# The last group of a split-fp32 down-projection: 28 additions moved from VectorE to transfers that add in SBUF

## The chip, the cores and the metric

The kernel runs on one core of one Trainium2 chip. A core has TensorE (matmuls, with a weight load per matmul), VectorE (elementwise work), ScalarE (activations, here mostly copies with a scale), GpSimd, SyncE (which here only issues transfers) and 16 DMA engines shared by all queues. The metric is the device time of one execution in microseconds.

## The reference, cut to what matters

One layer of a hybrid streaming encoder is computed for 512 prompt frames and 64 sample frames: a mixer, an output projection with a gated residual, and a gated feed-forward network (FFN) with its own gated residual, then a final norm. The change lies in the last three lines:

```python
x = x + g1 * mix                       # D_MODEL = 2048
h = rmsnorm(x, norm2[l]) * (1 + sc2) + sh2
f, s_f = conv_ffn(h, ffn_s[l], w_up[l], ffn_conv_w[l], ffn_conv_b[l], w_down[l])
x = x + g2 * f                         # f = act @ w_down, w_down (5632, 2048)
...
y = rmsnorm(x, final_norm)
```

`g2` is one gain per model column and per stream (prompt or sample). Everything is fp32.

## The kernel before, in words

Activations lie transposed: model columns on the 128 partitions, frames along the free dimension. A tile of 128 columns is kept as two halves `h`, each of 288 frames: 256 of the prompt and 32 of the sample (`HP` = 256, `HT` = 288; `HZ` = 290 has two extra columns between them, `ZS` = 258 is where the sample begins in it). An fp32 product is made of three matmuls: each operand is split into a high part (a copy by ScalarE to a rounded type) and a low part (the difference, by VectorE), and high x high, low x high and high x low are added up in PSUM.

**The norm stage** (lines 1190 to 1208). The first residual `x` is finished tile by tile while the output projection goes on. For each of the 16 tiles `norm_tile` squares `x`, stores `x` to DRAM (`xd[m]`, L1204, because it is wanted again at the very end), scales `x` in place for the second norm (L1206, ScalarE; this must wait for the store, which reads the same tile) and has GpSimd put two columns in the gap (L1207). The up-projection begins right behind the last tile; its first product is copied out by L1385 into `p`.

**The down-projection** multiplies `act` (44 tiles of 128 rows) by `w_down` (5632 x 2048). The first two of the 44 tiles go through plain products that also set the accumulators; the next 38 are paired and go through a Strassen-like scheme with 7 products instead of 8; the last four ("plain activations") go through plain products in `final`. The 38 make 19 pairs in 5 groups (3, 4, 4, 4, 4). A group has 4 blocks `q`, each of 512 of the 2048 output columns (two tiles of row half 0, two of row half 1), and each block has 7 steps `c`. A step of a group of four is 24 matmuls.

`down_prep` makes the weight split of a step two steps ahead: L1557 (ScalarE, high) and L1558 (VectorE, low), with sums of weight tiles before it on VectorE (L1551, L1568, L1578, L1583). Weights are loaded by SyncE (L1533) into six buffers used in turn, so a load waits until the split of the tile six loads before is made. The split tiles have three buffers in turn. After a step `down_out` adds the product from PSUM to an accumulator: to `acc[row, h][q]` (quarters of 128 x 2 x 288), or to `e0[q]` for product 0 (L1621 where it comes from two single banks, L1623 otherwise).

`e0` belongs in three of the four accumulators, so in the last group it is added to (1,1), (0,1) and (1,0) of each block by VectorE (L1698), after steps 1, 2 and 3. Then `down_finish` turns an accumulator into the new `x`: its pieces of the old `x` are loaded from `xd` (four issues, L1630), it is scaled by the gain `g2` on ScalarE (four activations, L1634), and the loaded `x` is added by VectorE (L1636). The four `(row, h)` of a block are begun after steps 1 to 4 of the block and added after its steps 4 to 7. The stage buffers for the loaded `x` and for the last plain activations are four tiles of the up-projection in turn (`stage`).

The last four plain activations are loaded (L1478) after step 4 of each block of the last group and split (L1484 ScalarE, L1485 VectorE) after step 6, so in steps 6, 13, 20 and 27 of the 28.

**The final part** begins right after step 27: for each half `h` and each of 16 tiles `m`, 12 matmuls with the last plain activations (L561, L563). Weight tiles come through the same six buffers and three split buffers for `m` below 6 (L648 load, L649, L650) and into free tiles above (L1780, L1783, L1784). `final_sum` (L1737, VectorE) adds the product with the gain to `x`; after every fourth tile `final_part` transposes the result on TensorE (L1810) and makes the last norm.

The order of instructions on each engine follows the program's order, changed by a planner of the framework that picks among ready instructions by the order of the program and by its own cost estimates; a few loads have a priority written by hand. `events[n]` in `down` is a list of calls made after step `n`.

Of the kernel before, what the change touches and what calls it, by code (L numbers as in the profile page):

```python
# [8 lines left out]
F32 = mybir.dt.float32  # L9
F32R = mybir.dt.float32r  # L10
I32 = mybir.dt.int32
AF = mybir.ActivationFunctionType
ALU = mybir.AluOpType
# [3 lines left out]
P = 128  # L17
D = 2048
KD = 16
TP, TS = 512, 64  # L20

HP, HS, HT = 256, 32, 288
NFF = 44
# [4 lines left out]
HZ, ZS = 290, 258  # L28
# [73 lines left out]
class Kern:  # L102
# [1091 lines left out]
    def norm_tile(self, m, first):  # L1194

        nc = self.nc
        A, x = nc.scalar, self.x1[m]
        if first:
            A.activation(self.sq, x, AF.Square)
        else:  # L1200
            t = self.xr()[:, :2 * HZ].rearrange("p (h t) -> p h t", h=2)
            A.activation(t, x, AF.Square)
            nc.vector.tensor_tensor(self.sq, self.sq, t, op=ALU.add)
        nc.sync.dma_start(self.xd[m], x)  # L1204
        for c, q in ((slice(0, HP), 0), (slice(ZS, HZ), 1)):
            A.activation(x[:, :, c], x[:, :, c], AF.Copy, scale=self.s2[:, m, q:q + 1])  # L1206
        nc.gpsimd.tensor_copy(x[:, 0, HP:ZS], self.mod[:, 3, m])  # L1207
# [402 lines left out]
    def down_out(self, step, c):  # L1610
# [11 lines left out]
        else:  # L1622
            V.tensor_tensor(out, (x, y)[(0, 1, 2, 0, 1, 2, 1)[c]], out, op=ALU.add)  # L1623

    def down_finish(self, row, h, q):

        nc, t, xt = self.nc, self.acc[row, h][q], self.stage()
        for a in range(2):
            for c, z in ((slice(0, HP), slice(0, HP)), (slice(HP, HT), slice(ZS, HZ))):
                nc.sync.dma_start(xt[:, a, c], self.xd[8 * row + 2 * q + a][:, h, z])  # L1630
        yield
        for a in range(2):
            for n, c in enumerate((slice(0, HP), slice(HP, HT))):
                nc.scalar.activation(t[:, a, c], t[:, a, c], AF.Copy, scale=self.g2[:, 8 * row + 2 * q + a, n:n + 1])  # L1634
        yield
        nc.vector.tensor_tensor(t, t, xt, op=ALU.add)  # L1636

    def down(self):
        A = self.nc.scalar
        free = [self.combos[c, j][2] for c in range(7) for j in range(NPAIR)]  # L1640
        take = lambda n: [free.pop(0) for _ in range(n)]
        self.combos, self.a, self.n_stage = {}, {}, 0
        self.raw = self.raw_late
        firsts = take(3 * FIRST)
        loads = [self.act_load(k, firsts[k]) for k in range(FIRST)]
        self.places = firsts[FIRST:]
        acts = [self.act_split(raw) for raw in loads]
        self.places = take(7 * GROUPS[0])
        quarters = lambda places: [self.slot(p, F32, HT) for p in places]
        self.acc = {}  # L1650
        for row in range(2):
            for h in range(2):
                self.acc[row, h] = quarters(take(4))
        self.e0_places = take(4)
        self.e0 = quarters(self.e0_places)
        spare = take(2 * GROUPS[0])
        self.places += free + firsts + spare
        self.g2 = self.sp.tile([P, KD, 2], F32, tag="g2", bufs=1, name="g2")
        for half, f in ((0, 1.0), (1, -1.0)):
            A.activation(self.g2[:, 8 * half:8 * half + 8], self.mod[:, 5, 8 * half:8 * half + 8], AF.Copy, scale=f)  # L1660

        steps = [((g, q), c) for g in range(len(GROUPS)) for q in range(4) for c in range(7)]
        blocks = [b for b, c in steps if c == 0] + [None]
        prep = lambda n: self.down_prep(*steps[n], blocks[n // 7 + 1]) if n < len(steps) else None
        raws = [self.pair_load(j, spare[2 * j:]) for j in range(GROUPS[0])]
        for m0 in range(0, KD, 4):
            wh, wl = self.wtile(self.i["w_down"][0, :FIRST * P, m0 * P:(m0 + 4) * P].rearrange("(k p) n -> p k n", p=P))
            if m0 == 4:
                self.down_load(blocks[0], ("a21", "a22"))
            if m0 == 8:  # L1670
                self.down_load(blocks[0], ("a11", "a12"))
                self.down_first(blocks[0])
            for m in range(m0, m0 + 4):
                ps = self.pgt()
                c = slice((m - m0) * P, (m - m0 + 1) * P)
                for k in range(FIRST):
                    self.mm6(ps, wh[:, k, c], wl[:, k, c], acts[k], k == 0, k == FIRST - 1)
                for h in range(2):
                    A.activation(self.acc[m // 8, h][m % 8 // 2][:, m % 2], ps[:, h, :HT], AF.Copy, scale=(1.0, -1.0)[m // 8])
            j = m0 // 4  # L1680
            if j < GROUPS[0]:
                for _ in self.down_pair(j, raws[j]):
                    pass
        for n in range(2):
            prep(n)

        last, acts, pairs = len(GROUPS) - 1, [], iter(())
        puts = {2: (1,) * 7, 3: (0, 3, 4, 4, 3, 4, 3)}
        events = [[] for _ in range(len(steps) + 1)]
        for q in range(4):  # L1690
            b = 7 * (4 * last + q)
            for i, (row, h) in enumerate(((0, 0), (1, 1), (0, 1), (1, 0))):
                f = self.down_finish(row, h, q)
                for at in (1, 3, 4):
                    events[b + i + at].append(lambda f=f: next(f, None))
            for c, (row, h) in enumerate(((1, 1), (0, 1), (1, 0)), 1):
                t = self.acc[row, h][q]
                events[b + c].insert(0, lambda t=t, e=self.e0[q]: self.nc.vector.tensor_tensor(t, t, e, op=ALU.add))  # L1698
            load = []
            events[b + 4].append(lambda q=q, load=load: load.append(self.act_load(NFF - 4 + q)))  # L1700
            events[b + 6].append(lambda load=load: acts.append(self.act_split(load.pop())))
        for n, (step, c) in enumerate(steps):
            g, q = step
            prep(n + 2)
            self.down_product(step, c)
            self.down_out(step, c)
            freed = lambda c: [self.combos[c, sum(GROUPS[:g]) + i][2] for i in range(GROUPS[g])]
            if q == 3 and c > 0:
                self.places += freed(c - 1)
            if g < last:  # L1710
                if (q, c) == (1, 6):
                    pairs = self.next_pairs(range(sum(GROUPS[:g + 1]), sum(GROUPS[:g + 2])))
                    next(pairs)
                for _ in range(puts[q][c] if q in puts else 0):
                    next(pairs)
            for f in events[n]:
                f()
            if q == 3 and c == 6:
                next(pairs, None)
                self.places += freed(c)  # L1720
        for f in events[-1]:
            f()
        self.final(acts, self.places + [])
# [110 lines left out]
def layer_kernel(tc, i, o):  # L1834
    nc = tc.nc
    with ExitStack() as ctx:
        K = Kern(tc, ctx, i, o)
        pool = lambda st, name, side="left", **kw: st.enter_context(tc.tile_pool(name=name, side=side, reuse_waits="tile", **kw))
        dp = ctx.enter_context(tc.tile_pool(name="dp", bufs=1, space=DRAM))
# [7 lines left out]
        K.zero3 = K.cp.tile([P, 3], F32, name="zero3")  # L1847
        nc.vector.memset(K.zero3, 0.0)
        K.xs = [dp.tile([P, 2, HT], F32, name=f"xs{k}") for k in range(KD)]
        K.xd = [dp.tile([P, 2, HZ], F32, name=f"xd{m}") for m in range(KD)]  # L1850
        K.actd = [dp.tile([P, 2, HT], F32, name=f"actd{t}") for t in range(NFF)]
        K.hp = pool(ctx, "hp", bufs=1)
        K.wq = pool(ctx, "wq", "right", bufs=3)
        with ExitStack() as early:
# [37 lines left out]
            z = [(K.zp, f"z{n}") for n in range(N_EXTRA)]  # L1892
# [98 lines left out]
```

## Time and profile before

| | us |
|---|---|
| three runs, median (lowest to highest) | 2870.66 (2866.38 to 2871.43) |
| profiled execution, whole | 2869.18 |
| its span, first to last instruction | 2867.4 |
| down-projection, last group (28 steps) | about 2695 to 2783.5 |
| final part | about 2783.5 to the end |

An instruction row gives engine, line, operation, output <- inputs, shapes, count, then the total busy time and the mean of one in ns, then the idle time of the engine before it and what ended it. A row of a stretch gives for each engine the busy time and in brackets the number of instructions, then the clock granted to TensorE (1.00 is full), the busy share of the 16 DMA engines and the rate in GB/s. A row of a single instruction in order of time gives its start, its duration, engine and line, with the idle time before it in square brackets. A row of a wait gives who waited for whom, the total in us, how many times and the longest. Busy times of two neighbouring instructions overlap a little, so the distance between two starts is what an instruction costs its engine.

### The profile page before, as it was taken

How to read it: one execution, taken by the hardware profiler on the slowest of the kernel's cores; microseconds unless marked ns; L12 is line 12 of the kernel's file. 1: busy time of each engine (PE TensorE's matmuls, PEld its weight loads, DVE VectorE, ACT ScalarE, POOL GpSimd, SP SyncE). 2: the span in 40 equal slices, each digit the busy share in tenths (PEclk: the TensorE clock that was granted, in tenths of full speed). 3: DMA queues.
4: the chain of work that ended last, by engine and by line, in shares of the span. 5: the costliest groups of instructions: out<-in, count | busy, mean ns of one | idle time of the engine just before them, and what ended most of it. 6: DMA issues, size and time to landing. Idle time of an engine off the chain costs nothing.

```text
span 2867.4 us, 52042 instructions
## 1 busy us (share of the span) xinstructions
PE 2810.4 (98%) x20596; PEld 2708.7 (94%) x20596; DVE 2301.9 (80%) x3742; ACT 1355.0 (47%) x2379; POOL 320.6 (11%) x587
## 2 busy tenths in 40 slices
PE   7999999999999999999999999999999999999998
PEld 3599999999999999999999999999999999999997
DVE  5788878777778777468888888888887889999995
ACT  7574566544333333255444444444444464434453
POOL 0005432224310001001000000000000000000000
PEclk9999999999999999999999999999999999999999
DMA  9975555545455448433333333333333343443451
GB/s 308 306 209 148 157 149 161 158 140 152 129 166 172 146 131 251 123 119 102 102 101 102 108 106 108 102 108 108 101 101 105 105 150 114 123 127 118 126 169 67
DMA packets 522441, 399.80 MB, mean 139 GB/s; under 512 B 50793, under 2 KB 453956, under 8 KB 522196
## 3 DMA queue, kind: packets, MB, share of 16 engines
q1 hardware_dynamic: 516772, 385.79, 45.3%
q0 software_dynamic: 5424, 10.68, 1.2%
q8 instruction: 162, 2.65, 0.4%
q14 instruction: 83, 0.68, 0.1%
HBM read 356.24 MB, written 40.13 MB: 138 GB/s over the span
## 4 chain that ended last, share of the span: by engine, by line
PE 82%; DVE 9%; DMA 3%; ACT 3%; issue 2%; SPq 0%; POOL 0%; ACTq 0%; DVEq 0%
PE g L561 19%; PE g L563 10%; PE g L1373 9%; PE g L1374 8%; PE g L1375 8%; PE bank L1374 3%; PE bank L1373 3%; PE bank L1375 3%; DVE wl L1558 2%; PE g L1606 2%; PE g L1608 2%; PE g L1607 2%; DMA raw<-in_w_down_dram 1%; PE bank L162 1%; PE bank L826 1%
## 5 line engine op out<-in xcount | busy, mean ns | idle before, releaser
L1373 PE MATMUL g<-slot,wh 128*128 128x290 f32 x1760 | 534.2, 304 | 2.4 <-ACT p L1385 2.4
L1374 PE MATMUL g<-slot,wh 128*128 128x290 f32 x1760 | 526.6, 299 | 0.0
L1375 PE MATMUL g<-slot,wl 128*128 128x290 f32 x1760 | 520.9, 296 | 0.0
L561 PE MATMUL g<-hh,wh 128*128 128x288 f32 x1984 | 450.4, 307 | 2.4 <-ACT hh L1160 1.3
L561 PE MATMUL g<-hl,wh 128*128 128x288 f32 x1984 | 432.3, 298 | 0.0
L563 PE MATMUL g<-hh,wl 128*128 128x288 f32 x1984 | 432.0, 298 | 0.0
L1320 ACT ACTIVATE wh<-raw 128x1024 fp32r<-128x1024 f32 x176 | 186.8, 1061 | 393.1 <-PE g L1374 376.8
L1373 PEld LDWEIGHTS g<-slot,wh 128*128 128x128 f32 x1760 | 331.8, 189 | 16.9 <-ACT p L1385 11.3
L1375 PEld LDWEIGHTS g<-slot,wl 128*128 128x128 f32 x1760 | 337.2, 192 | 0.0
L1374 PEld LDWEIGHTS g<-slot,wh 128*128 128x128 f32 x1760 | 335.6, 191 | 0.1
L561 PEld LDWEIGHTS g<-hh,wh 128*128 128x128 f32 x1984 | 319.1, 190 | 5.6 <-ACT hh L1160 1.5
L561 PEld LDWEIGHTS g<-hl,wh 128*128 128x128 f32 x1984 | 321.3, 189 | 0.3
L563 PEld LDWEIGHTS g<-hh,wl 128*128 128x128 f32 x1984 | 319.6, 189 | 0.2 <-issue 0.2
L649 ACT ACTIVATE wh<-raw 128x1024 fp32r<-128x1024 f32 x163 | 172.6, 1059 | 309.1 <-PE g L561 272.6
L650 DVE TENSOR_TENSOR wl<-raw,wh 128x1024 fp32r<-128x1024 f32 x163 | 199.1, 1222 | 52.8 <-ACT wh L649 50.9
L820 DVE SCALAR_TENSOR_TENSOR acc<-xr,ct,acc 128x512 f32<-128x512 f32 x322 | 230.4, 751 | 1.5 <-DMA xr<-in_w_ada_dram 1.5
L1321 DVE TENSOR_TENSOR wl<-raw,wh 128x1024 fp32r<-128x1024 f32 x176 | 214.8, 1220 | 19.3 <-ACT wh L1320 19.2
L1606 PE MATMUL g<-slot,wh 128*128 128x288 f32 x760 | 224.8, 296 | 2.3 <-DVE slot L1623 1.1
L1608 PE MATMUL g<-slot,wl 128*128 128x288 f32 x760 | 224.4, 296 | 0.3 <-DVE wl L1558 0.3
L1607 PE MATMUL g<-slot,wh 128*128 128x288 f32 x760 | 224.4, 295 | 0.0
L1374 PE MATMUL bank<-slot,wh 128*128 128x290 f32 x704 | 210.3, 299 | 0.0
L1373 PE MATMUL bank<-slot,wh 128*128 128x290 f32 x704 | 209.6, 298 | 0.0
(416 smaller groups left out, 6083.0 us busy)
## 6 DMA issues: line engine op xcount, KB each, us to landing
raw<-in_w_up_dram SPq DMA_DIRECT2D x176, 512.0 KB, 4.0
raw<-in_w_in_dram SPq DMA_DIRECT2D x108, 512.0 KB, 3.9
xr<-in_w_ada_dram SPq DMA_DIRECT2D x86, 512.0 KB, 3.9
raw<-in_w_down_dram SPq DMA_DIRECT2D x76, 512.0 KB, 3.6
ax<-in_w_ada_dram SPq DMA_DIRECT2D x42, 512.0 KB, 3.7
hraw<-in_w_ada_dram SPq DMA_DIRECT2D x40, 512.0 KB, 9.5
raw<-in_w_out_dram SPq DMA_DIRECT2D x32, 512.0 KB, 4.3
raw<-in_w_ada_dram SPq DMA_DIRECT2D x24, 512.0 KB
```

The costliest lines, as they stand in the source:

```text
L561: T.matmul(ps[:, h if bank is None else bank, :n], wh, x[:, h, :n], start=f, stop=False)
L563: T.matmul(ps[:, h if bank is None else bank, :n], wl, ah[:, h, :n], start=False, stop=stop)
L650: nc.vector.tensor_tensor(lo[:, :n_], raw[:, :n_], hi[:, :n_].bitcast(F32), op=ALU.subtract)
L820: V.scalar_tensor_tensor(acc[s], w[:, k], col, acc[s], op0=ALU.mult, op1=ALU.add)
L1320: self.nc.scalar.activation(hi, src, AF.Copy)
L1321: self.nc.vector.tensor_tensor(lo, src, hi.bitcast(F32), op=ALU.subtract)
L1373: T.matmul(ps, wh[:, j], hi, start=(c < 3 and j == 0), stop=False, skip_group_check=True)
L1374: T.matmul(ps, wh[:, j], lo, start=False, stop=False, skip_group_check=True)
L1375: T.matmul(ps, wl[:, j], hi, start=False, stop=(j == NPAIR - 1), skip_group_check=True)
L1606: T.matmul(ps, wh[:, j, f], hi, start=(c < 3 and j == 0), stop=False, skip_group_check=True)
L1607: T.matmul(ps, wh[:, j, f], lo, start=False, stop=False, skip_group_check=True)
L1608: T.matmul(ps, wl[:, j, f], hi, start=False, stop=(j == n - 1), skip_group_check=True)
```

## The change

Four things change.

- `e0` and the old `x` are added to the accumulators in the last group by transfers that GpSimd issues, with addition as the operation on their target in SBUF (`down_add`). There are 12 for `e0` (after steps 0, 1 and 4 of a block: to (1,0), (0,1), (1,1)) and 16 for `x`. The additions on VectorE, the loads of `x` into stage buffers and their issues on SyncE go.
- The scaling by `g2` and the addition of `x` come after steps 3, 5, 6 and 7 of a block, for (0,0), (0,1), (1,1), (1,0); the scaling waits for the `e0` transfer, the `x` transfer for the scaling.
- The old `x` is kept in DRAM by quarters, in the layout of the accumulators, so that one transfer of 128 x 576 adds a quarter. The norm stage therefore stores each tile in four pieces (two halves, prompt and sample) instead of one.
- The last plain activations are loaded into one buffer of the up-projection (tag `g`), after steps 0, 6, 12 and 18 of the last group's 28, and split after steps 3, 9, 15 and 21.

```diff
@@ norm_tile
-        nc.sync.dma_start(self.xd[m], x)
+        for h in range(2):
+            for c, z in ((slice(0, HP), slice(0, HP)), (slice(HP, HT), slice(ZS, HZ))):
+                nc.sync.dma_start(self.xq[m // 8, h][m % 8 // 2][:, m % 2, c], x[:, h, z])
@@
+    def down_add(self, row, h, q, src):
+        self.nc.gpsimd.dma_start(self.acc[row, h][q], src, accum_op=ALU.add)
+
     def down_finish(self, row, h, q):
 
-        nc, t, xt = self.nc, self.acc[row, h][q], self.stage()
-        for a in range(2):
-            for c, z in ((slice(0, HP), slice(0, HP)), (slice(HP, HT), slice(ZS, HZ))):
-                nc.sync.dma_start(xt[:, a, c], self.xd[8 * row + 2 * q + a][:, h, z])
-        yield
+        t = self.acc[row, h][q]
         for a in range(2):
             for n, c in enumerate((slice(0, HP), slice(HP, HT))):
-                nc.scalar.activation(t[:, a, c], t[:, a, c], AF.Copy, scale=self.g2[:, 8 * row + 2 * q + a, n:n + 1])
-        yield
-        nc.vector.tensor_tensor(t, t, xt, op=ALU.add)
+                self.nc.scalar.activation(t[:, a, c], t[:, a, c], AF.Copy, scale=self.g2[:, 8 * row + 2 * q + a, n:n + 1])
+        self.down_add(row, h, q, self.xq[row, h][q])
@@ down
         for q in range(4):
             b = 7 * (4 * last + q)
-            for i, (row, h) in enumerate(((0, 0), (1, 1), (0, 1), (1, 0))):
-                f = self.down_finish(row, h, q)
-                for at in (1, 3, 4):
-                    events[b + i + at].append(lambda f=f: next(f, None))
-            for c, (row, h) in enumerate(((1, 1), (0, 1), (1, 0)), 1):
-                t = self.acc[row, h][q]
-                events[b + c].insert(0, lambda t=t, e=self.e0[q]: self.nc.vector.tensor_tensor(t, t, e, op=ALU.add))
-            load = []
-            events[b + 4].append(lambda q=q, load=load: load.append(self.act_load(NFF - 4 + q)))
-            events[b + 6].append(lambda load=load: acts.append(self.act_split(load.pop())))
+            for at, (row, h) in ((0, (1, 0)), (1, (0, 1)), (4, (1, 1))):
+                events[b + at].append(lambda row=row, h=h, q=q: self.down_add(row, h, q, self.e0[q]))
+            for at, (row, h) in ((3, (0, 0)), (5, (0, 1)), (6, (1, 1)), (7, (1, 0))):
+                events[b + at].append(lambda row=row, h=h, q=q: self.down_finish(row, h, q))
+            load, b = [], 28 * last + 6 * q
+            events[b].append(lambda q=q, load=load: load.append(self.act_load(NFF - 4 + q, (self.ub, "g"))))
+            events[b + 3].append(lambda load=load: acts.append(self.act_split(load.pop())))
@@ layer_kernel
-        K.xd = [dp.tile([P, 2, HZ], F32, name=f"xd{m}") for m in range(KD)]
+        K.xq = {(r, h): [dp.tile([P, 2, HT], F32, name=f"xq{r}{h}{q}") for q in range(4)] for r in range(2) for h in range(2)}
```

## The prediction

> **What bounds the kernel now.** I read the page first, then the stretch that the change touches block by block, then what TensorE waits for in it, then VectorE's order at its end.
>
> ```profile
> PE 2810.4 (98%) x20596; PEld 2708.7 (94%) x20596; DVE 2301.9 (80%) x3742; ACT 1355.0 (47%) x2379; POOL 320.6 (11%) x587
> ```
>
> TensorE is busy 98% of the span, so nothing can be won except where it stands still or runs at a lower clock. VectorE's 80% is an average; the four blocks of the last group of the down-projection (7 steps each) show it differently:
>
> ```profile
> core 0: us, PE busy (x) PEld busy (x) DVE busy (x) ACT busy (x) POOL busy (x), PEclk, DMA share, GB/s
> 2695.00:2717.10 22.10, 22.10 (x169) 22.10 (x168) 22.10 (x30) 10.16 (x20) 0.00 (x0) 1.00 0.47 136
> 2717.10:2739.20 22.10, 22.10 (x167) 21.97 (x166) 22.10 (x29) 12.05 (x23) 0.00 (x0) 1.00 0.60 164
> 2739.20:2761.30 22.10, 21.67 (x160) 21.11 (x159) 21.94 (x28) 11.79 (x23) 0.00 (x0) 1.00 0.59 162
> 2761.30:2783.50 22.20, 22.20 (x170) 22.19 (x169) 21.81 (x28) 13.83 (x28) 0.00 (x0) 1.00 0.70 207
> ```
>
> In the last group VectorE is full (22.10 of 22.10 us) while TensorE still keeps its pace, 168 matmuls in 22.1 us, 0.131 us each and 24 x 0.131 = 3.15 us a step. VectorE just fails to keep up; what it falls behind is eaten from the two steps by which the weight splits run ahead. TensorE pays only when that lead is gone: some 8 matmuls are missing in the third block (160), and the rest of the bill comes where the group hands over to the final part. What TensorE waited for from 2690 us to the end:
>
> ```profile
> PE bank L1810 <- DVE slot L1737: 3.0, 1, 3.0
> PE g L561 <- DVE slot L1485: 0.8, 1, 0.8
> PE g L1606 <- ACT wh L1557: 0.3, 1, 0.3
> ```
>
> Both long waits are for VectorE: L1485 is the split of the last plain activation, L1737 the final part's first sums. VectorE's own order there:
>
> ```profile
> 2786.34 0.75 DVE L1485 TENSOR_TENSOR slot<-raw,slot 128x576 fp32r<-128x576 f32 x1
> 2787.01 1.22 DVE L650 TENSOR_TENSOR wl<-raw,wh 128x1024 fp32r<-128x1024 f32 x1
> 2788.14 0.75 DVE L1636 TENSOR_TENSOR slot<-slot,raw 128x576 f32<-128x576 f32 x1
> 2788.81 0.48 DVE L1800 COPY v<-bank 88x128 f32<-88x128 f32 x2
> 2789.21 1.28 DVE L1784 TENSOR_TENSOR hw<-raw,hw 128x512 fp32r<-128x512 f32 x2
> 2790.41 1.19 DVE L1737 SCALAR_TENSOR_TENSOR slot<-g,mod,slot 128x256 f32<-128x256 f32 x4
> ```
>
> An addition of the old form (L1636) holds VectorE from 2788.14 to 2788.81, 0.67 us. It stands, with other late work, in front of the sums (L1737) that TensorE waits for. After the wait the clock has fallen:
>
> ```profile
> 2775.00:2780.00 5.00, 5.00 (x40) 5.00 (x40) 4.74 (x7) 5.00 (x11) 0.00 (x0) 1.00 0.98 334
> 2785.00:2790.00 5.00, 2.17 (x15) 1.70 (x13) 4.34 (x8) 5.00 (x13) 0.00 (x0) 0.97 0.44 151
> 2790.00:2795.00 5.00, 4.06 (x17) 4.07 (x18) 3.25 (x9) 1.96 (x4) 0.00 (x0) 0.50 0.06 17
> 2795.00:2800.00 5.00, 5.00 (x33) 4.96 (x33) 3.93 (x11) 0.00 (x0) 0.00 (x0) 0.84 0.00 0
> ...
> 2792.14 0.68 PE L561 MATMUL g<-slot,wh 128*128 128x288 f32 x2
> 2792.86 0.68 PE L561 MATMUL g<-slot,wh 128*128 128x288 f32 x2
> ...
> 2796.47 0.48 PE L561 MATMUL g<-slot,wh 128*128 128x288 f32 x2
> ...
> 2797.31 0.43 PE L561 MATMUL g<-slot,wh 128*128 128x288 f32 x2
> 2797.70 0.42 PE L561 MATMUL g<-slot,wh 128*128 128x288 f32 x2
> ```
>
> The column before the last two is the granted clock: 0.50, then 0.84. Three matmuls take 0.72 us (2792.14 to 2792.86) where they take 0.39 us at full clock (2797.31 to 2797.70). That lasts from about 2791, when the sums of 2790.41 are there, to 2796.47, where a pair takes 0.48 us again: some 7 such triples, 7 x 0.33 = 2.3 us lost.
>
> **Part by part: what is there to gain.** 0.8 us (wait for L1485), 3.0 us (wait for L1737), 2.3 us (clock) and the third block's 7 to 10 missing matmuls x 0.131 = 0.9 to 1.3 us, of which I take 0.9, since records can be missing: 7.0 us. More than this the stage can't give, for TensorE is otherwise at its pace.
>
> **VectorE.** Twenty-eight additions of 128x576 leave it, 12 of e0 (L1698) and 16 of x (L1636):
>
> ```profile
> L1636 DVE TENSOR_TENSOR slot<-slot,raw x16: 748/762/778, 2711.9 to 2788.1; 128x576 f32<-128x576 f32 x16
> L1698 DVE TENSOR_TENSOR slot<-slot,slot 128x576 f32<-128x576 f32 x12 | 9.2, 767 | 0.0
> ```
>
> They are all of one shape, so 0.67 us of queue each: 28 x 0.67 = 18.8 us, 4.7 us in a block of 22.1. VectorE then has about 17.4 us of work per block; its lag is gone after the first block. The lag also held back SyncE, because weight buffers come free with the VectorE split; with it goes the third block's loss. The last split (L1485) moves from step 27 to step 21 of 28, six steps or 19 us sooner, and its load passes only weight loads on SyncE's queue; its buffer is one that nothing else uses by then. What is late next at the handover? The third final weight tile takes the buffer that the group's last step frees, at 2783.5; its ScalarE copy (1.06 us, as L1320 below has it for that shape) and VectorE split (L650, 1.22 us) end near 2786, and TensorE wants it after two tiles of 24 matmuls, 2 x 3.15 us, at 2789.8. Nothing is late by that.
>
> **SyncE.** It loses 64 issues of x pieces in the last group and gains 48 store issues in the norm stage (1215 to 1311 us):
>
> ```profile
> L1630 SPq DMA_DIRECT2D raw<-xd x64: 319/430/1716, 2688.0 to 2769.4; - x64
> L1204 SPq DMA_DIRECT2D xd<-slot x16: 319/338/339, 1215.5 to 1310.5; - x16
> DMA to landing us min/median/max: 2.5/2.5/2.5
> ```
>
> Each norm tile now stores four pieces instead of one, so its in-place scaling (L1206) waits for three more issues, 3 x 0.43 = 1.3 us at the most. For 15 tiles work of the next tiles covers that. For the last it meets a place where TensorE stands:
>
> ```profile
> 1310.46 0.32 SPq L1204 DMA_DIRECT2D xd<-slot  x1
> 1312.53 1.06 ACT L1320 ACTIVATE wh<-raw 128x1024 fp32r<-128x1024 f32 x1 [0.71 <-PE g L1374]
> 1313.49 0.94 ACT L1206 ACTIVATE slot<-slot,s 128x512 f32<-128x512 f32 x2
> 1315.35 0.39 ACT L1385 ACTIVATE p<-g 128x290 f32<-128x290 f32 x1
> 1315.79 0.61 PE L1373 MATMUL g<-slot,wh 128*128 128x290 f32 x1 [2.24 <-ACT p L1385]
> ```
>
> The store landed at 1310.46 + 2.5 = 1313.0 and ScalarE came to L1206 at 1313.49. The third of four pieces, issued 0.86 us later, lands at 1313.9; L1206 slips 0.4 us, and p (L1385) and TensorE behind it. Taken: +0.4 us; between nothing and 1.3. Below nothing too: should the planner now put p ahead of L1206, up to 2.2 us come back.
>
> **GpSimd's queue and the transfers.** It is idle in this stage (POOL 0.00) and gets 28 transfers of 128x576x4 = 295 KB, each adding into its target. The trace has none that adds; the nearest rows are GpSimd's plain stores of 256 KB and its queue as a whole:
>
> ```profile
> L1002 POOL DMA_DIRECT2D od<-m x16: 667/674/1441, 286.2 to 1114.7; - x16
> DMA to landing us min/median/max: 2.5/3.7/5.4
> ...
> q0 software_dynamic: 5424, 10.68, 1.2%
> ```
>
> An issue takes 0.67 to 1.44 us, seven to a block 5 to 10 of 22.1 us. 1.2% of 2867 us for 10.68 MB is 0.95 us of all engines for 295 KB. That is the lower end for an addition; the upper is 5.4 us, the longest landing, if each had to end before the next began. Nearer to the first, since the queue overlaps its transfers, I take 1.9 us, twice a plain one, because the target is read as well. Seven transfers may take 22.1 us, 3.16 us each, before they queue up. The engines' share, 0.47 to 0.70, then rises by (28 x 1.9 - 16 x 0.95) / 88.5 = 0.43 less whatever overlaps, near full but not over it. Who waits: step 6's scaling of (1,1) waits for the e0 transfer issued after step 4, 6.3 us earlier, and behind it in ScalarE's queue are the weight copies, which run two steps ahead, 6.3 - 1.06 - 1.22 = 4.0 us to spare. So a landing of up to about 10 us, less 0.77 for the sum before it, costs nothing; the rows show 3.7, at most 5.4. Cost taken: 0.
>
> The Trainium skill, page "Collectives: The Full Stack", section "The bandwidth ceiling: the fold count and why AG ≠ RS ≠ AR", speaks against adding in a transfer: a reduce reads two sources on one ring and so moves at about half a copy's rate. No run here shows it yet; by that page the estimate is 2 x 0.95 = 1.9 us for one transfer, under the 3.16 us, and the sum would be the same -6.6 us.
>
> **Sum.** -7.0 + 0.4 = -6.6 us from the profiled execution, 2869.18 us (span 2867.4 and 1.8 around it): 2862.6 us. That execution lies 1.5 us under the median of the three runs, 2870.66, and 2.8 over the fastest. About 0.2%, 5.7 us, is what a measurement tells from no change, so the forecast stands just beyond it.
>
> **The rivals.** *The handover stays.* ScalarE is full there too (5.00 of 5.00 us twice above), and the engines were at 0.98 while the final weights came; the added transfers fall into just that stretch. If ScalarE or a late load takes VectorE's place, the 3.0 and the 2.3 us stay, and only 0.8 + 0.9 - 0.4 = 1.3 us is won: 2867.9. For it: those two rows. Against: the x pieces and one activation load leave that stretch, and SyncE is freed early. *The adding transfers become the bound* (slower). If one holds the queue for more than 3.16 us, the rest pile up. At 4 us each, between the 1.9 taken and the 5.4, the lag is 28 x 0.84 = 23.5 us at the group's end; 10 us are covered, ScalarE and then TensorE wait for the other 13.5: 2869.18 - 6.6 + 13.5 = 2876.1. It decides above 3.16 us, over three times a plain transfer's 0.95. Against: that factor. For: no row shows an addition. *The change does nothing*: VectorE's relief is not on the path; excluded by the waits, which name L1485 and L1737, except for noise.
>
> **How the numbers follow.** Forecast 0.62, handover stays 0.29, transfers bound 0.09. Of the forecast's own spread (2859 to 2865) a tenth falls inside 0.2%, and so does the whole second case: faster 0.55, same 0.36, slower 0.09. The range takes the p gain and the spread of the runs below (2862.6 - 2.2 - 1.9 = 2858.5) and the second case with the median's 1.5 us above (2867.9 + 1.5 = 2869.4).
>
> **What would show it.** Right: no L1636 or L1698 on VectorE; its busy time near 17.4 us in each of the four blocks; 168 matmuls in the third; no wait for L1737 or L1485, clock 1.00 through the handover; adding transfers landing in under 10 us; TensorE's wait for p at 2.2 to 3.5 us. Wrong: ScalarE waiting for transfers before L1634 for longer than 4 us, weight loads landing later than 10 us, or a handover wait of 3 us with another releaser.

## The result, and the profile after

The changed kernel takes 2883.75 us, the median of 6 runs (2881.65 to 2889.97); the kernel before takes 2868.55 us, the median of its 6. The ratio is 1.0056, with a 95% interval of 1.0043 to 1.0069: slower. The forecast of 2862.6 us was wrong in sign.

The profiled execution has a span of 2881.0 us against 2867.4, 13.6 us more. Cut at the first up-projection matmul, the last one, the start of the last group and the start of the final part (by the trace the group before began at 2692.9, not at 2695):

| stretch, us | before | after | difference |
|---|---|---|---|
| up to the first up-projection matmul | 1309.2 | 1313.3 | +4.1 |
| up-projection | 1019.0 | 1017.1 | -1.9 |
| from there to the last group | 364.7 | 365.3 | +0.6 |
| last group of the down-projection | 90.7 | 104.7 | +14.0 |
| final part to the end | 83.8 | 80.6 | -3.2 |

The loss lies in the stretch that was to gain. The first row is one execution against one: in all kernels below that stretch took between 1305.8 and 1314.6 us. I give it to no part of the change, and where it comes from stays open.

The page's line of busy times, of the changed kernel:

```profile
PE 2815.7 (98%) x20596; PEld 2710.6 (94%) x20596; DVE 2283.2 (79%) x3714; ACT 1356.3 (47%) x2379; POOL 348.7 (12%) x615
```

The 28 additions are gone from VectorE (3742 to 3714 instructions) and are 28 instructions more on GpSimd. TensorE is at 98% as before; at that resolution the loss isn't seen. The four blocks of the last group show it, in the columns of the prediction (busy time and count for each engine, granted clock, share of the DMA engines, GB/s):

```profile
2695.65:2717.89 22.24, 22.24 (x171) 22.24 (x170) 21.21 (x30) 10.17 (x15) 3.53 (x4) 1.00 0.66 159
2717.89:2743.24 25.35, 22.50 (x171) 22.29 (x169) 21.17 (x25) 14.72 (x30) 6.30 (x8) 1.00 0.84 188
2743.24:2769.72 26.48, 24.02 (x171) 23.81 (x169) 18.43 (x22) 12.19 (x23) 6.66 (x8) 0.94 0.79 162
2769.72:2800.38 30.66, 25.15 (x173) 24.57 (x171) 14.78 (x19) 12.21 (x23) 5.27 (x7) 0.89 0.72 163
```

The blocks are cut here where TensorE begins them. Four blocks without a stall take 89.1 us (run e1 below), 22.3 each; the second takes 3.1 us more, the third 4.2 and the fourth 8.4. VectorE is no longer full, least of all in the fourth block. The transfer engines nearly are: 0.84 and 0.79 for whole blocks. And TensorE stands still in each of the three, as its waits from 2680 us on say. (Line numbers are those of each run's own kernel: L1625, L1559 and L1734 here are L1623, L1557 and L1737 before.)

```profile
PE g L1608 <- DVE slot L1625: 5.3, 2, 2.9
PE bank L1608 <- ACT wh L1559: 5.0, 1, 5.0
PE bank L1807 <- DVE slot L1734: 1.9, 1, 1.9
PE g L561 <- DVE slot L1625: 1.8, 1, 1.8
```

The first two lines are new: matmuls of the group itself wait, for VectorE's addition that frees their PSUM (L1625) and for ScalarE's weight copy (L1559). Both engines have room, so why are they late? Their own waits answer:

```profile
ACT hw L1780 <- DMA raw<-in_w_down_dram: 14.8, 2, 9.9
...
DVE s L1570 <- DMA raw<-in_w_down_dram: 8.2, 2, 4.8
```

Both stand at the head of their queues for a weight load. In order of time, VectorE in the second block (start, duration, in brackets the idle time before and its end):

```profile
2731.51 0.75 DVE L1625 TENSOR_TENSOR slot<-g,slot 128x576 f32<-128x576 f32 x1
2735.66 1.23 DVE L1570 TENSOR_TENSOR s<-s,raw 128x1024 f32<-128x1024 f32 x1 [3.39 <-DMA raw<-in_w_down_dram]
2736.80 1.22 DVE L1560 TENSOR_TENSOR wl<-raw,wh 128x1024 fp32r<-128x1024 f32 x1
2737.93 1.22 DVE L1580 TENSOR_TENSOR raw<-raw,raw 128x1024 f32<-128x1024 f32 x1
2739.07 0.75 DVE L1625 TENSOR_TENSOR slot<-g,slot 128x576 f32<-128x576 f32 x1
```

and TensorE behind it:

```profile
2739.97 0.37 PE L1608 MATMUL g<-slot,wh 128*128 128x288 f32 x1 [2.85 <-DVE slot L1625]
```

A sum of weight tiles (L1570), for a later step, is put ahead of the addition at 2739.07, which empties the PSUM that TensorE needs now. The sum waits for its load, two more operations for later steps follow, and the addition comes last. ScalarE does the same in the fourth block: two copies of a final weight tile (L1780) stand ahead of the group's own weight copies (L1559), first ScalarE, then TensorE:

```profile
2777.71 1.04 ACT L1559 ACTIVATE wh<-raw 128x1024 fp32r<-128x1024 f32 x1
2788.61 1.15 ACT L1780 ACTIVATE hw<-raw 128x512 fp32r<-128x512 f32 x2 [9.86 <-DMA raw<-in_w_down_dram]
2789.67 1.04 ACT L1559 ACTIVATE wh<-s 128x1024 fp32r<-128x1024 f32 x1
```

```profile
2790.76 0.61 PE L1608 MATMUL bank<-slot,wh 128*128 128x288 f32 x1 [5.00 <-ACT wh L1559]
```

The loads they wait for, in the chain that ended last (start, time, what):

```profile
2729.09 6.47 DMA raw<-in_w_down_dram
...
2753.32 6.53 DMA raw<-in_w_down_dram
...
2778.05 10.48 DMA raw<-in_w_down_dram
...
2794.93 8.29 DMA slot<-slot
```

Three weight loads, one per late block, and at the end one adding transfer of `e0`. In the chain of the kernel before, the two weight loads of this stage took 5.9 us each. After the stalls of the third and the fourth block the clock is down too, 0.50 in the 5 us from 2790; in the second block it stays at 1.00, as the rows of the blocks show.

```profile
2780.00:2785.00 5.00, 5.00 (x40) 5.00 (x39) 1.39 (x2) 0.00 (x0) 0.45 (x1) 1.00 1.06 234
2785.00:2790.00 5.00, 0.77 (x6) 0.53 (x5) 0.72 (x2) 1.39 (x3) 0.00 (x0) 0.96 0.73 215
2790.00:2795.00 5.00, 3.72 (x14) 3.38 (x15) 4.54 (x6) 3.89 (x7) 0.61 (x2) 0.50 0.32 79
```

The three waits sum to 5.3 + 5.0 = 10.3 us of the group's 14.0; the lowered clock of the third and fourth block (0.94 and 0.89) is part of the rest, which I don't take apart. In the first of these rows the transfer engines are at 1.06, full by this measure, while ScalarE does nothing (0.00) but wait for them.

The theories, then. **T1**: the adding transfers fill the engines, and the weight loads, which share them, land late. **T2**: the planner, which orders by its own estimates, now puts work that waits for a load ahead of work that is ready, so a late load becomes a stall of TensorE. **T3**, the rival: the activation loads, which now come six steps sooner, block the weight loads on SyncE's queue.

### The profile page after: what moved, and what is told of

It is laid out like the page before. It is cut to its first block, busy times and chain, and to the rows that moved or that the text cites. A ratio compares the mean times of both kernels' runs of the same rounds, so it can differ in the third digit from the quotient of the medians.

```text
span 2881.0 us, 52075 instructions
## 1 busy us (share of the span) xinstructions
PE 2815.7 (98%) x20596; PEld 2710.6 (94%) x20596; DVE 2283.2 (79%) x3714; ACT 1356.3 (47%) x2379; POOL 348.7 (12%) x615
## 4 chain that ended last, share of the span: by engine, by line
PE 82%; DVE 7%; DMA 4%; ACT 4%; issue 2%; SPq 0%; POOL 0%; ACTq 0%; DVEq 0%; POOLq 0%
PE g L561 19%; PE g L563 9%; PE g L1375 9%; PE g L1376 8%; PE g L1377 8%; PE bank L1376 3%; PE bank L1375 3%; PE bank L1377 3%; PE g L1608 3%; PE g L1610 3%; PE g L1609 3%; PE bank L162 1%; DVE acc L820 1%; PE bank L1608 1%; PE bank L1609 1%
```

## The experiments

All ratios are to the kernel before, timed beside it. "Group" and "final" are the last two stretches of the table above, in the profiled execution of each (before: 90.7 and 83.8).

### The transfers: none, plain, half as wide

```diff
 # e1_no_add
-        self.nc.gpsimd.dma_start(self.acc[row, h][q], src, accum_op=ALU.add)
+        pass
 # e2_plain_copy
+        self.nc.gpsimd.dma_start(self.acc[row, h][q], src)
 # e9_half_width
+        self.nc.gpsimd.dma_start(self.acc[row, h][q][:, 0], src[:, 0], accum_op=ALU.add)
```

> The changed kernel with its 28 adding transfers left out (so e0 and the old x are missing in the output); all else stays, the early activation loads and the order of work too. Theory T1, the transfers fill the DMA engines and weight loads land late: the stalls of the last group go and the handover gain stays, about 2861 us, 8 under before. Theory T2, the planner's new order puts work that waits for weight loads ahead of ready work: the stalls stay, 2875 us or more. Theory T3, the earlier activation loads through one buffer block SyncE and ScalarE: 2875 us or more.

> The changed kernel with the 28 transfers as plain copies that overwrite their target instead of adding to it (the sums are lost); issues, queue and waits are the same. T1: engine time per transfer falls from 1.9 us to about 0.95, so about half of the loss goes, 2868 to 2874 us. T2 and T3: within 0.1 to 0.2% of the changed kernel, 2880 us or more.

> The changed kernel with each of the 28 adding transfers cut to half its columns (128x288; the other half of each sum is left out of the output). Issues, queue, waits and order stay. If the engine time of the adding is what delays the weight loads (1.86 us of all engines each, so 0.93 here): 0.999 to 1.002 of before, like the plain copies. If the number of transfers and the chain scale, transfer, scale behind them make the loss: 1.004 or more.

| | ratio, 95% | median us | group | final |
|---|---|---|---|---|
| e1, no transfer | 0.9978 (0.9969 to 0.9988) | 2860.39 | 89.1 | 78.8 |
| e2, plain copies | 1.0009 (0.9998 to 1.0020) | 2870.29 | 90.8 | 84.5 |
| e9, half the columns | 1.0004 (0.9993 to 1.0016) | 2869.22 | 90.1 | 84.2 |
| changed, 28 full additions | 1.0056 (1.0043 to 1.0069) | 2883.75 | 104.7 | 80.6 |

The transfer engines' time by queue, from 2690 to 2800 us (packets, MB, share of the 16 engines; q0 is GpSimd's queue, q1 that of the loads), changed kernel, e2 and e9 in turn:

```profile
q0 software_dynamic: 3468, 7.12, 40.9%
q1 hardware_dynamic: 9979, 10.84, 31.5%
```

```profile
q1 hardware_dynamic: 10710, 11.46, 33.7%
q0 software_dynamic: 2240, 8.26, 22.1%
```

```profile
q1 hardware_dynamic: 10710, 11.46, 33.2%
q0 software_dynamic: 4032, 4.13, 25.7%
```

An addition of 295 KB takes 0.409 x 110 us / (7.12 / 0.295) = 1.86 us of all engines (24 of the 28 fall into this window); a plain copy 0.221 x 110 / 28 = 0.87; an addition of half the bytes 0.257 x 110 / 28 = 1.01. So the price goes nearly with the bytes and is 2.1 times that of a copy. The Trainium skill, page "Collectives: The Full Stack", section "The bandwidth ceiling: the fold count and why AG ≠ RS ≠ AR", gives a reduction, which reads two sources, about half the rate of a copy; the 2.1 of this trace agrees.

Halving that time, by either way, takes the group's 14 us away, with all 28 issues still on GpSimd; e9 even keeps their cost per issue (0.87 us as in the changed kernel, 0.54 in e2). The weight loads go the same way. Counting packets of q1 from the issue of a load until its 512 KB are through (an estimate, since most landings aren't recorded), the loads of this window take 3.6 us in the median and 5.7 at the longest before, 4.9 and 9.0 in the changed kernel, 4.1 and 6.0 in e2, 3.8 and 6.1 in e9, 3.1 and 4.4 in e1. That is T1.

Without any transfer the kernel is 6.5 us faster, about what was predicted; whether VectorE's relief earns that is taken up with e8. With e2 and e9 the gain isn't there, and TensorE's longest waits from 2680 us on say where it went; e1, e2, e9:

```profile
PE g L561 <- DVE slot L1625: 1.8, 1, 1.8
```

```profile
PE g L561 <- ACT slot L1635: 4.2, 1, 4.2
```

```profile
PE g L561 <- ACT wh L649: 5.9, 1, 5.9
```

The handover to the final part is won only in e1. In the other two ScalarE has taken VectorE's place: the group is as long as before and the final part too (84.5, 84.2). That is the prediction's rival "the handover stays". One difference stays between e1 and the rest: it has no waits for additions either, so its gain isn't that of the lighter engines alone.

### The early activation loads

```diff
 # e3_act_late: the changed kernel with
-            load, b = [], 28 * last + 6 * q
-            events[b].append(lambda q=q, load=load: load.append(self.act_load(NFF - 4 + q, (self.ub, "g"))))
-            events[b + 3].append(lambda load=load: acts.append(self.act_split(load.pop())))
+            load = []
+            events[b + 4].append(lambda q=q, load=load: load.append(self.act_load(NFF - 4 + q)))
+            events[b + 6].append(lambda load=load: acts.append(self.act_split(load.pop())))
 # e4_act_early_only: the kernel before with the reverse of these lines, and nothing else
```

> The changed kernel with the last plain activations loaded and split where they were before (after steps 4 and 6 of each block, in the stage buffers). T3: the loss goes, 2862 to 2868 us. T1 and T2: 2880 us or more.

> The kernel before with only the activation loads and splits moved to every sixth step and one buffer. T3: 2878 us or more. T1 and T2: 2865 to 2870 us, as before or a little better, since VectorE's split of the last activation comes 19 us sooner.

e3 is at 1.0051 (1.0035 to 1.0067), as slow as the changed kernel; e4 at 0.9997 (0.9988 to 1.0007), as fast as the kernel before. T3 falls, and the early loads by themselves are worth nothing that can be measured. (In e4's profile the group is 1.5 us longer, 92.2, and the final part 3.2 shorter, 80.6.)

### The order

`issue_after` has the planner put what is inside it behind the given instruction. Applied to the weight splits and sums of the last group, it keeps them behind the addition that frees PSUM; the second edit takes the hand-written priority from the copies of the final weights (their loads keep it).

```diff
 # e10_dve_order, and e5_order
-            prep(n + 2)
+            if g == last:
+                with self.tc.issue_after(out_of):
+                    prep(n + 2)
+            else:
+                prep(n + 2)
...
             self.down_out(step, c)
+            out_of = self.nc.cur_bb.bb.instructions[-1]
 # e11_hw_order, and e5_order: these lines move out of "with ...high_priority(offset=AHEAD)"
+        for j, (hi, lo) in enumerate(w):
+            r = raw[:, :, j * P:(j + 1) * P]
+            self.nc.scalar.activation(hi, r, AF.Copy)
+            self.nc.vector.tensor_tensor(lo, r, hi.bitcast(F32), op=ALU.subtract)
```

> The changed kernel, all 28 adding transfers kept, with the order mended by hand: in the last group a step's weight preparation on VectorE is queued behind the addition of the product three steps before it, and the final part's copies of weights (L1780) lose their priority. T1, the adding transfers fill the DMA engines, whatever the order: within 0.2% of the changed kernel, 1.004 to 1.007 of before. T2, the loss is that ready work stands behind work that waits for a load: at least half of it goes, 1.002 of before or less.

> Only the first half of the mended order: VectorE's weight preparation in the last group queued behind the addition three steps before. If the additions that free PSUM (TensorE's waits for L1625, 5.3 us and the 1.8 at the end) are the larger part: 1.003 of before or less; if ScalarE's wait for the final part's loads is: 1.004 or more.

> Only the second half: the final part's weight copies (L1780) without their priority. ScalarE's waits for those loads (14.8 us in the changed kernel, 9.9 the longest) no longer stand ahead of the last group's own copies. If they are the larger part: 1.003 of before or less; if not, 1.004 or more.

| | ratio, 95% | median us | group | final |
|---|---|---|---|---|
| e10, first edit | 1.0031 (1.0019 to 1.0043) | 2875.92 | 97.2 | 81.8 |
| e11, second edit | 1.0052 (1.0037 to 1.0067) | 2881.96 | 108.2 | 80.7 |
| e5, both | 1.0020 (1.0011 to 1.0029) | 2873.72 | 96.6 | 83.0 |

In e5 the transfers are the same 28, all within the window now, and cost nearly what they did: 0.459 x 110 / 28 = 1.80 us each. The loads are late as well, 4.8 us in the median and 7.8 at the longest by the count above. Yet some two thirds of the loss are gone. Its TensorE waits (L1739 and L1785 are L1734 and L1780 of the changed kernel):

```profile
PE g L561 <- DVE slot L1739: 3.9, 2, 3.6
PE bank L1608 <- ACT wh L1559: 3.8, 1, 3.8
```

The waits for L1625 (5.3 us) are no more, in e10 too: the late loads became stalls of the second and third block through VectorE's order. That is T2 for VectorE. T2 alone isn't enough: e1 has the order of the changed kernel in these places (L1570, L1560 and L1580 ahead of the addition; on ScalarE L1780 ahead of the group's last L1559) and no stall, because its loads are in time: L1570 waits 0.40 us for its load there, against 3.39. In the kernel before, both sums (L1568, L1578) come behind that addition, and the final copies (L1783) behind the last L1557: the order changed with the edit. The wait in the fourth block remains, and so does its cause, in ScalarE's row of e5:

```profile
2776.39 1.15 ACT L1785 ACTIVATE hw<-raw 128x512 fp32r<-128x512 f32 x2 [6.99 <-DMA raw<-in_w_down_dram]
```

The planner puts the final copies ahead even without the priority (e11: 9.45 us of the same wait). The second edit thus didn't do what it was meant to: e11 stands at the changed kernel's ratio, e5 and e10 overlap, and that ScalarE's order makes the fourth block's stall is read from the trace, not shown by a run.

### Some of the additions only

```diff
 # e6_e0_only: 12 of e0 by transfer; the old x is loaded two steps sooner into a stage buffer, in one load, and
-        self.down_add(row, h, q, self.xq[row, h][q])
+        self.nc.vector.tensor_tensor(t, t, xt, op=ALU.add)
 # e7_x_only: 16 of x by transfer; e0 on VectorE
-                events[b + at].append(lambda row=row, h=h, q=q: self.down_add(row, h, q, self.e0[q]))
+                events[b + c].insert(0, lambda t=t, e=self.e0[q]: self.nc.vector.tensor_tensor(t, t, e, op=ALU.add))
 # e8_vector_xq: both edits, so no adding transfer, but x by quarters and the early activation loads
 # e12_x_only_order: e7 and both edits of e5
```

> Only the 12 additions of e0 by adding transfers; the old x is loaded from its quarters in one plain load each and added by VectorE. T1 with a price per transfer: no additions at all gave -0.22%, 28 adding transfers +0.56%, so 12 of 28 with 8 us of VectorE saved lie between, 0.999 to 1.002 of before. A special price on the e0 transfers (ScalarE's scaling waits for them: 6.4 us in the changed kernel) would show as 1.003 or more.

> Only the 16 additions of the old x by adding transfers; e0 is added by VectorE as before. T1 with a price per transfer: 1.000 to 1.003 of before. If the waits of ScalarE for e0 make the loss instead: 0.998 or less.

> All 28 additions on VectorE, with the old x kept by quarters (64 stores in the norm stage, 16 loads of one piece in the last group) and the early activation loads. The prediction's +0.4 us for the norm stage: 0.999 to 1.001 of before, with TensorE's wait for p between 2.2 and 3.5 us. If the stores by pieces cost or save more, it shows here alone: a wait for p of under 1 us would mean that the planner put p ahead.

> Only the old x by adding transfers (16), e0 on VectorE, with both halves of the mended order. If lateness of loads and order together are the whole loss, the group comes to about 89 us and the tail to 80: 0.998 of before, the fastest complete kernel so far. If the order mended by hand costs something of its own: 0.999 or more, as with 16 adding transfers in the planner's order (0.9992).

| | additions by transfer | ratio, 95% | median us | group | final |
|---|---|---|---|---|---|
| e8 | 0 | 0.9988 (0.9976 to 1.0000) | 2863.70 | 91.9 | 79.4 |
| e6 | 12 | 1.0001 (0.9989 to 1.0012) | 2869.04 | 95.3 | 81.7 |
| e7 | 16 | 0.9992 (0.9983 to 1.0002) | 2865.81 | 91.4 | 81.7 |
| e12 | 16, with order | 0.9998 (0.9988 to 1.0007) | 2868.58 | 91.7 | 82.3 |
| changed | 28 | 1.0056 (1.0043 to 1.0069) | 2883.75 | 104.7 | 80.6 |

Twelve or sixteen cost nothing and bring nothing that can be told from no change; twenty-eight cost 0.56%. The cost isn't one per transfer; it sets in when the engine time that has to fit into the group is large. Share times length, that time is 53 us before, 55 in e2, 57 in e9, 58 in e7, 70 in e6 and 79 in the changed kernel, of a group that takes 89.1 us without a stall; the groups are 90.7, 90.8, 90.1, 91.4, 95.3 and 104.7 us long. e6 stands between, with a longer group and no loss that can be told in the whole. In e7 the loads take 4.2 us in the median and 6.2 at the longest by the count above, and the order, which had mended most of the loss with 28, does nothing with 16 (e12). e8 is the best of the kernels that compute the whole layer, by 0.12% with an interval that reaches 1.

e8 also bears on e1. It leaves VectorE all 28 additions, and yet its final part is 4.4 us shorter than before, against 5.0 in e1. The wait for the final part's first sums (L1740 here) is nearly what it was, 3.0 us before, but the clock stays full behind it where it had fallen to 0.50 (the row is the second 5 us of the final part; in e4, behind a wait of 2.3 us at the same place, the clock is 0.69 there, so what decides it stays open):

```profile
PE bank L1813 <- DVE slot L1740: 2.5, 1, 2.5
2786.47:2791.47 5.00, 4.08 (x31) 4.08 (x32) 4.79 (x13) 1.49 (x3) 0.00 (x0) 1.00 0.05 12
```

Group and final part together are 174.5 us before, 171.3 in e8 and 167.9 in e1, in one execution each. So about half of e1's gain in these two stretches comes without VectorE's relief, and the ratios of e1 and e8 overlap (0.9969 to 0.9988, 0.9976 to 1.0000): what the relief alone is worth, up to some 3.4 us, is not shown.

### The additions on GpSimd itself

If the engines are the trouble, the additions could be GpSimd's elementwise work, without transfers.

```diff
 # e13_gpsimd_all: all 28; e14_gpsimd_x: 16 of x; e15_gpsimd_e0: 12 of e0; the others on VectorE
-        self.nc.gpsimd.dma_start(self.acc[row, h][q], src, accum_op=ALU.add)
+        self.nc.gpsimd.tensor_tensor(self.acc[row, h][q], self.acc[row, h][q], src, op=ALU.add)
```

> All 28 additions as elementwise work on GpSimd, at the places of the changed kernel; the old x loaded from its quarters, one plain load each. If the relief of VectorE is worth what the prediction said and only the adding transfers spoilt it: 0.998 of before. If the chain of waits behind the additions takes it back: 1.000 or more. GpSimd's time for one is not shown by any run so far; above about 3.1 us (88 us for 28) it would become the bound, 1.002 or more, and if it slows VectorE's own two-input work, VectorE's rows of 0.75 and 1.22 us grow.

> The 16 additions of x on GpSimd as elementwise work, e0 on VectorE. Relief theory: about 16/28 of the gain, 0.9985 of before. Chain theory: 1.000.

> The 12 additions of e0 on GpSimd as elementwise work, x loaded in one piece and added by VectorE. Relief theory: 12/28 of the gain over all on VectorE, 0.998 to 0.999 of before. Chain theory (ScalarE's scaling waits for e0): 1.000 or more.

In the order e13, e14, e15 the ratios are 1.0051 (1.0036 to 1.0066), 1.0022 (1.0010 to 1.0033) and 1.0021 (1.0007 to 1.0035), the groups 104.8, 98.2 and 99.2 us. All three are slower than the kernel before, though VectorE has 28, 16 and 12 additions less. VectorE's groups of e13 in this stretch (count, busy us, mean ns, idle before) show why:

```profile
L1560 DVE TENSOR_TENSOR wl<-raw,wh 128x1024 fp32r<-128x1024 f32 x15 | 22.9, 1530 | 1.9 <-ACT wh L1559 1.9
...
L1625 DVE TENSOR_TENSOR slot<-g,slot 128x576 f32<-128x576 f32 x20 | 14.9, 746 | 0.2 <-PE g L1610 0.2
L1585 DVE TENSOR_TENSOR s<-raw,s 128x1024 f32<-128x1024 f32 x4 | 8.8, 2188 | 0.0
```

In the changed kernel the same operations take 1217, 749 and 1221 ns. What reads both inputs from SBUF (L1560, L1585) has grown by a quarter to four fifths; what reads one from PSUM (L1625) has not. Within e13, too, the ten of L1560's 27 with no GpSimd addition beside them take 1.21 to 1.22 us and the others up to 2.45, while L1625 takes 0.74 to 0.76 either way. The Trainium skill, page "SBUF — State Buffer", section "Who interferes with whom", says that such VectorE operations and GpSimd's reads of SBUF get in each other's way; the rows agree, with these sizes. So these runs bring another cost in and can't say what VectorE's relief alone would be worth.

## Why the prediction was wrong, point by point

- **The failed step** is "Cost taken: 0" in the part on GpSimd's queue and the transfers. Its price was right (1.9 us estimated, 1.86 measured) and its queue bound too: 7 x 1.86 = 13.0 us in a block of 22.1 don't pile up. What failed is the conclusion from "near full but not over it", and by the step's own sum it didn't follow: 0.43 on top of 0.47 to 0.70 is 0.90 to 1.13, over full in the fourth block. The step asked only who waits for the adding transfers; it didn't ask who shares the engines with them. The weight loads do: those on the path of the late blocks took 6.5, 6.5 and 10.5 us, where the same chain has 4.7 and 4.8 in e1 and 5.9 before. The price, with the new order of VectorE's and ScalarE's queues, was the group's 14.0 us.
- **The rival "adding transfers become the bound"** got the side right, but by another mechanism: it needed over 3.16 us for a transfer, and the loss came at 1.86.
- **The landing bound**, "a landing of up to about 10 us ... costs nothing", was made for the order of the kernel before. The adding transfers landed in 3.5 to 9.1 us, inside it, and ScalarE's scaling still waited for them:

```profile
ACT slot L1635 <- DMA slot<-slot: 6.4, 3, 3.7
```

  The order of the queues, which the bound took as given for every step, had changed; with VectorE's order mended 0.25 (e10) to 0.36 (e5) of the 0.56% are gone.
- **The gain**, 7.0 us: e1 comes within half a microsecond of it, but that is in part luck. The group could give more than the 0.9 taken: a step takes 3.18 us in e1, not 3.15, and e1's group is 1.6 us shorter than before. By e8, VectorE's relief can be about half of e1's gain in the two stretches (3.4 of 6.6 us), and the wait for p below is gone in e1 too, where a loss was forecast. In the changed kernel the wait for the last split is gone, the wait for the final part's first sums shrank from 3.0 to 1.9 us (L1807 above), the clock stays at 1.00 through the handover as forecast, and 1.8 us for L1625 came at the same place. Its final part is 3.2 us shorter; so is that of e4, which takes nothing from VectorE, so this isn't shown to be the relief either.
- **VectorE**: the additions left, but its busy time isn't "near 17.4 us in each of the four blocks". It is 21.21, 21.17, 18.43 and 14.78, in sum 75.6 us against 90.1 for the whole group before: 14.5 less, not 18.8. Two of the 28 additions had stood behind the group's end, and four splits of final weight tiles (2.7 us) were drawn forward into it.
- **SyncE in the norm stage**: the sign was wrong, and the lower bound that was named came true: ScalarE now makes p ahead of the last scaling. TensorE's wait of 2.2 us for p is there in the kernel before and in e4 (2.3 us), which keep x as before, and in none of the kernels that store it by quarters. From the up-projection's start (1309.2 before, 1313.3 after) TensorE is busy for 7.76 us of 10 before and 9.41 after. The row after:

```profile
1313.30:1323.30 10.00, 9.41 (x64) 8.40 (x63) 10.00 (x23) 7.56 (x17) 3.83 (x4) 1.00 0.65 178
```

- **Of its signs of being wrong** one came in full: a weight load beyond 10 us (10.48). The handover has a wait with another releaser (L1625), but of 1.8 us, not 3, and ScalarE's longest wait for a transfer is 3.7 us, not over 4.

What stays open: whether any kernel with all its sums can have e1's 6.5 us, and how much of them is VectorE's relief; how much of the fourth block's stall an order of ScalarE's queue would take away; and the 4.1 us ahead of the up-projection.

## What to carry to other kernels

An operation moved from an engine to transfers is paid for by whoever else uses the transfer engines: add up their shares with the new transfers, and when a stage comes near full (two blocks stood at 0.84 and 0.79 here), ask which loads land later and what is queued behind the instruction that waits for them. Price the order as well as the work: the order changed here, and work drawn forward that waits for a load held up what was ready. A removed wait at a handover is only won if the next engine in line (in e2 and e9 ScalarE) is early as well. And a gain of the forecast size doesn't show the forecast cause: e1 alone would have seemed to confirm the relief, and e8 has half of e1's gain without it.

## What the runs showed of the hardware

- A transfer that adds into SBUF takes 2.1 times the engine time of a plain one of the same bytes (1.86 against 0.87 us for 295 KB), and its issue holds GpSimd for 0.87 us against 0.54. Changed kernel, then e2 (least, median and most in ns):

```profile
L1628 POOL DMA_DIRECT2D slot<-xq x16: 857/868/871, 2712.2 to 2807.6; - x16
```

```profile
L1628 POOL DMA_DIRECT2D slot<-xq x16: 537/537/539, 2708.7 to 2791.8; - x16
```

- GpSimd adds 128x576 fp32 values in 1.6 to 2.2 us, two to three times VectorE's 0.75, and while it does, VectorE's operations on two SBUF inputs take up to 1.8 times as long (2188 against 1221 ns):

```profile
L1628 POOL TENSOR_TENSOR slot<-slot,slot 128x576 f32<-128x576 f32 x12 | 26.8, 2240 | 380.6 <-DVE slot L1625 380.6
L1639 POOL TENSOR_TENSOR slot<-slot,raw 128x576 f32<-128x576 f32 x16 | 25.7, 1607 | 42.3 <-ACT slot L1637 35.3 <-DMA raw<-in_w_down_dram 4.0 <-DMA raw<-xq 1.5
```
